# A two-layer mixture-of-experts kernel: the slot table by one-hot products, slots given out by age, fp32r transposes of gathered rows

## The chip, the cores and the metric

The kernel runs on one core of a Trainium2 chip. The metric is device time in microseconds (us): the median of three runs, 1536.97 us for the kernel before (1535.93 to 1539.32). One more execution was profiled; all rows below are from it.

## The reference

Two layers over 512 tokens of width 1024, all in fp32. Each layer mixes tokens (two kinds of attention, then an output projection), normalises, and runs 16 experts, of which each token uses two. The experts are what the change touches:

```python
def grouped_moe(x, w_router, router_bias, exp_w_gate, exp_w_up, exp_w_down):
    xf = x.reshape(b * s, d)                                   # 512 x 1024
    scores = sigmoid(einsum('nd,de->ne', xf, w_router))        # 512 x 16
    biased = scores + router_bias
    group_score = lax.top_k(biased.reshape(n, 4, 4), 2)[0].sum(-1)
    in_group = (arange(16) // 4)[None, :] == argmax(group_score, -1)[:, None]
    _, idx = lax.top_k(where(in_group, biased, -inf), 2)       # two experts a token
    w = take_along_axis(scores, idx, -1); w = w / w.sum(-1, keepdims=True)
    combine = sum(one_hot(idx, 16) * w[..., None], axis=1)
    y = zeros_like(xf)
    for e in range(16):
        h = silu(xf @ exp_w_gate[e]) * (xf @ exp_w_up[e])      # 1024 -> 512, twice
        y = y + combine[:, e:e + 1] * (h @ exp_w_down[e])      # 512 -> 1024
    return y
...
for l in range(2):
    x = layer_norm(alpha * x + token_mixer(x, ...), ln1_g[l], ln1_b[l])
    x = layer_norm(alpha * x + grouped_moe(x, ...), ln2_g[l], ln2_b[l])
```

The kernel computes an expert for its own tokens only: up to 128 of them, packed into one tile.

## The kernel before

**Products.** An fp32 product is made of three fp32r products (`mm3`, L454): each operand is split into a high part, cast by ACT (L484), and a low part, the rest subtracted by DVE (L495). An expert has 12 weight loads of 512 KB (128x1024), so 12 casts and 12 subtractions of 128x1024 stand beside its products: gate and up (24 records of 128x512 each per 512 outputs, 48 in all) and down.

**Routing.** The output projection yields the four tiles of 128 tokens one after the other. For each, `route_tile` (L1095) picks the two experts on DVE as one-hot rows `oh`, and gets from small bf16 products on PE (weights `lstr`, `ones`) the rank of every token among its expert's tokens. Rank and expert make a row number `ri` of the slot table; two scatters on POOL (L1153) write token number and weight there, in the DRAM table `tabd`. `route_end` (L1164) counts the tokens of each expert, then reads 128 slots x 16 experts of the table back into SBUF by one DMA on SP's queue, into the tile `tb` (in the trace `m<-tabd`). `tb` gives expert e's token numbers and weights.

**Experts.** `moe` (L1240) runs them in order. Expert 0's tokens are fetched by a one-hot product on PE (into two PSUM banks, `xacc`), which needs no table. Experts 1 to 15 are gathered by an indirect DMA on POOL's queue (L1179) from `x1d` in DRAM with a column of `tb`; eight transposes on PE (L445) turn such a tile, ACT and DVE split it. The result of an expert is scaled and added into `zd` in DRAM by an indirect scatter (L1184), except the last one, which `ln2` adds by a one-hot product. `ln2` begins with four reads of `zd` on SP's queue (`s<-zd`). Behind expert 14 stands `overflow` (L1190), a conditional block for experts of more than 128 tokens; it is skipped with this data, yet its buffers and its DMAs' semaphores take part in the plan.

**Order and slots.** No order is written by hand. Operations are recorded, and `plan` (L175) plays them through a model of the engines: the planned start sets the order on each engine. It also gives every tile a slot: 48 slots of 4 KB (`s`), 56 small ones (`m`), 8 tiny ones (`t`), 4 + 4 PSUM banks (`p`, `a`). `take` (L269) sorts the free slots by the time at which they came free and, among those free at the planned time, picks the newest. A tile that gets a slot waits on the chip for every reader and writer of the tile before it there.

Of the kernel before, what the change touches and what calls it, by code (L numbers as in the profile page):

```python
# [22 lines left out]
P = 128  # L23
# [68 lines left out]
class Recorder:  # L92
# [82 lines left out]
    def plan(self):  # L175
# [93 lines left out]
        def take(o, t):  # L269
            for b in o.allocs:  # L270
                s = slots[b.kind]
                s.sort()
                i = max((j for j in range(len(s)) if s[j][0] <= t + 1e-9), default=0)
                b.slot = s.pop(i)[1]
                g = b.group
                if g is not None:
                    if live[g] >= self.QUOTA[g]:
                        heapq.heappop(glive[g])
                        live[g] -= 1
                    live[g] += 1  # L280
                    turn[g].pop()
# [138 lines left out]
class Chip:  # L420
# [13 lines left out]
    def mm(self, out, terms, start, stop, transpose=None, also=()):  # L434
        dt = {F: 4, FR: 1, BF: 1}
        n = self.n(out)
        if transpose is not None:
            dur = 0.11
        else:
            dur = sum(max(dt[x.dtype if not isinstance(x, View) else x.ap.dtype] * n, 256) / 2400 + 0.004 for _, x in terms)  # L440

        def fn():
            o = real(out)
            if transpose is not None:
                self.nc.tensor.transpose(o, real(transpose[0]), transpose[1])  # L445
            for i, (w, x) in enumerate(terms):
                self.nc.tensor.matmul(o, real(w), real(x), start=start and i == 0, stop=stop and i == len(terms) - 1)  # L447
        reads = [x for t in terms for x in t] + ([transpose[0]] if transpose else [])
        o = self.r.add("PE", dur, fn, [out], reads, allocs=also)
        o.cols = sum(n * w.shape[0] / P for w, _ in terms) + n * (transpose is not None)  # L450
        o.cnt = sum(2 if (x.ap.dtype if isinstance(x, View) else x.dtype) == F else 1 for _, x in terms) + (transpose is not None)
        return o
# [91 lines left out]
def build(tc, x0, xT0, w_idx, w_main, w_br, w_out, w_exp, bgate, idxg, idxb,  # L544
          ln1g, ln1b, ln2g, ln2b, wrt, rbias, ln1c, hconst, tab0, out):
    nc = tc.nc
    with ExitStack() as ctx:
# [19 lines left out]

        ident = const.tile([P, P], F, name="ident")
        make_identity(nc, ident)
        identb = const.tile([P, P], BF, name="identb")  # L570
# [23 lines left out]
        rowid = const.tile([P, P], F, name="rowid")  # L594
        nc.gpsimd.iota(rowid, pattern=[[NE, P]], base=1, channel_multiplier=0, allow_small_or_imprecise_dtypes=True)
        spacer = const.tile([1, 1], F, name="spacer")

# [6 lines left out]
        def sm(shape, dtype=F):  # L604
            return R.buf("m", shape, dtype)
# [9 lines left out]
        lnc = const.tile([P, DEPTH, 2, KD], F, name="lnc")  # L615
        onesf = const.tile([P, P], F, name="onesf")
        nc.vector.memset(onesf, 1.0)
# [60 lines left out]

        def transpose_tile(src, dst_of):
            for hb in range(2):  # L680
                ps = bank("a")
                for k in range(4):
                    c = (hb * 4 + k) * P
                    C.tr(ps[:, k * P:(k + 1) * P], src[:, c:c + P], ident)
                dst_of(hb, ps)
# [408 lines left out]

        def route_tile(t, rt, sc, scored, sels, oh0, xacc):  # L1095
            bi = sm([P, NE])
# [39 lines left out]
            else:  # L1136
                for f in later + [pick]:
                    f()
                later.clear()
            o2, ri = sm([P, 2, NE]), R.buf("t", [P, 2], I32)  # L1140
            C.tt(o2, oh, pr[:, None, :NE].to_broadcast([P, 2, NE]), OP.mult)
            C.v("reduce_max", ri, o2, axis=AX.X, n=2 * NE)
            ent, o3, w2, rw = R.buf("t", [P, 2, 2], I32), sm([P, 2, NE]), sm([P, 2]), sm([P, 2])
# [4 lines left out]
            C.v("reciprocal", rw[:, 1:2], rw[:, 0:1])  # L1148
            last = C.ts(ent[:, :, 1:2].bitcast(F), w2[:, :, None], rw[:, 1:2], 1.0 / ALPHA, OP.mult, OP.mult)
            for j in range(2):  # L1150
                def scatter(j=j):
# [11 lines left out]

        def route_end(sels):  # L1164
            pc = bank("a")
            for tt in range(NT):
                C.mm(pc[:, :NE], [(ones, sels[tt])], tt == 0, tt == NT - 1)
            mc, mci = sm([P, 1]), sm([P, 1], I32)
            C.v("reduce_max", mc, pc[:, :NE], axis=AX.X, n=NE)
            C.v("tensor_copy", mci, mc)  # L1170
            tb, gl = sm([P, NE, 2], I32), sm([P, 2], I32)
            o = C.dma(tb, tabd[0:P * NE, :].rearrange("(r e) w -> r e w", e=NE), P * 160, rtok=["tab0"])
            o.deps.update(table_writes)
            C.ts(gl[:, 0:1], tb[:, NE - 1, 0:1], float(S - 1), None, OP.min)
            return tb, gl, mci

# [13 lines left out]
        def overflow(l, mci):  # L1190
# [45 lines left out]

            o = R.add("ALL", 0.3, fn, reads=[mci], rtok=[f"x1{t}" for t in range(NT)] + ["tab0", "y"], allocs=bufs)
            written.append(o)

        def moe(l, tb, gl, mci, loads, xacc, until, routed):  # L1240
            def prep(e):
# [5 lines left out]
                if e == 0:  # L1247
# [4 lines left out]
                    return xh, xl  # L1252
                xg = s4([P, D], group="xg")
                last = e == NE - 1
                gather(xg, gl[:, 0:1] if last else tb[:, e, 0:1], [xh, xl], not last)
                transpose_tile(xg, dst)
                return xh, xl
# [31 lines left out]
            def down(e, sg):  # L1289
# [16 lines left out]
                def scaled(n, ps):  # L1306
                    C.mul(yo[:, half(n)], ps, tb[:, e, 1:2].bitcast(F))
                    if lo is not None:
                        C.stt(lo[:, half(n)], ps, tb[:, e, 1:2].bitcast(F), yo[:, half(n)].bitcast(F), OP.mult, OP.subtract)
                def whole(n):  # L1310
                    w = weights(e, 4 + n)
                    ps = bank("p")
                    product(ps, w, range(4))
                    scaled(n, ps)
                    if n:
                        add_rows(tb[:, e, 0:1], yo)
                if lo is None:
# [44 lines left out]
            oh, tf = s4([P, NT, P], FR), sm([P, NT])  # L1362
            C.stt(tf, tb[:, NE - 1, 0:1].to_broadcast([P, NT]), float(NE), tilerow, OP.mult, OP.add).deps.add(mark)
            for t in range(NT):
# [75 lines left out]
        for l in range(DEPTH):  # L1440
# [53 lines left out]
            table_writes.clear()  # L1494
            sels, oh0, xacc = [], s4([P, NT, P]), [bank("p") for _ in range(2)]
            caps = [(None, CAP0), (R.ops[-2], CAP1)]
            rw, rsum, rcon = router_rows(l)
            for t, r, sc, scored, until in out_proj(l, mts, pair, x0 if l == 0 else x2d, None if l == 0 else "x2", rw, rsum, rcon):
                if t == 0:
                    caps.append((until, CAP2))  # L1500
                routed = route_tile(t, r, sc, scored, sels, oh0, xacc)
            caps.append((until, None))
            tb, gl, mci = route_end(sels)
            tail = moe(l, tb, gl, mci, expert_loads(l, caps), xacc, caps[2][0], routed)
        ln2(DEPTH - 1, None, tail)
# [84 lines left out]
```

## Time and profile before

| | |
|---|---|
| runs | 1536.97 us, median of 3 (1535.93 to 1539.32) |
| profiled execution | 1539.54 us, its span 1537.7 us |
| PE busy | 1475.2 us (96%) |
| DVE busy | 1249.5 us (81%) |
| ACT busy | 896.6 us (58%) |
| POOL busy | 142.4 us (9%) |
| mean granted TensorE clock | 0.983 |

PE is busy but for 62.5 us of the span (1537.7 - 1475.2). The span outside is 1.84 us. In rows of the trace, `p` and `a` are PSUM banks, `s`, `m` and `t` the slot pools; `out<-in` names the tiles; a bracket at a row's end holds the idle time ahead of it and what ended it. PEclk 1.00 is 2.4 GHz, and a stretch between 0.5 and 1 holds times at 1.2 GHz. Experts run from about 449 to 750 us in layer 0 and from about 1210 to 1512 us in layer 1.

### The profile page before, as it was taken

The page shows a single profiled execution, that of the slowest core. Times are in us where ns is not written, and L with a number is a line of the kernel's source. Part 1 is how long each engine was busy: PE and PEld are TensorE (multiplying, and loading weights), DVE is VectorE, ACT ScalarE, POOL GpSimd, SP SyncE. Part 2 cuts the span into 40 slices and gives each one's busy share as a digit, 9 for nine tenths or more (in the row PEclk, how much of TensorE's full clock was granted, in tenths as well). Part 3 has the DMA queues.
Part 4 walks back from the last instruction along what each step waited for, and adds up shares of the span by engine and source line. Part 5 has one row for each costly group of instructions (what it writes and reads, how often), then busy time and mean ns, then how long its engine had stood idle before and what let it go on. Part 6 is the DMA issues. An engine that isn't in the chain of part 4 may idle for free. (4 is left out here: it accounts for less than half of the span.)

```text
span 1537.7 us, 21018 instructions
## 1 busy us (share of the span) xinstructions
PE 1475.2 (96%) x7188; PEld 1178.9 (77%) x7188; DVE 1249.5 (81%) x2301; ACT 896.6 (58%) x1459; POOL 142.4 (9%) x127
## 2 busy tenths in 40 slices
PE   8999999999989999999799999999999899999985
PEld 7877777777867878888588777777778578888874
DVE  5699996777587989999765999867766789999975
ACT  4335543675146878888623455446831478888873
POOL 0000000000031131210010000000001212112110
PEclk9999999999999999999999999999999899999998
DMA  6221112117888989999712221221287889999962
GB/s 217 71 91 57 68 56 89 63 42 288 302 280 297 337 309 348 341 334 333 237 61 69 83 61 50 82 83 55 70 306 279 302 307 351 341 352 339 351 216 108
DMA packets 91265, 308.52 MB, mean 201 GB/s; under 512 B 15439, under 2 KB 15567, under 8 KB 91152
## 3 DMA queue, kind: packets, MB, share of 16 engines
q1 hardware_dynamic: 82000, 290.69, 53.5%
q0 software_dynamic: 9152, 16.43, 4.5%
q8 instruction: 58, 0.95, 0.2%
q14 instruction: 55, 0.45, 0.1%
HBM read 293.80 MB, written 28.46 MB: 210 GB/s over the span
## 5 line engine op out<-in xcount | busy, mean ns | idle before, releaser
L447 PE MATMUL p<-s,s 128*128 128x512 f32 (+1 forms) x5192 | 1268.1, 398 | 28.1 <-DVE s L495 25.7
L447 PEld LDWEIGHTS p<-s,s 128*128 128x128 f32 x5192 | 952.9, 191 | 234.9 <-DVE s L495 25.5
L495 DVE TENSOR_TENSOR s<-s,s 128x1024 fp32r<-128x1024 f32 (+2 forms) x526 | 612.1, 1195 | 152.4 <-ACT s L484 112.3
L484 ACT CAST s<-s 128x1024 fp32r<-128x1024 f32 (+2 forms) x526 | 518.2, 1029 | 226.6 <-PE p L447 141.6
L495 DVE TENSOR_TENSOR s<-a,s 128x256 fp32r<-128x256 f32 (+3 forms) x386 | 169.5, 479 | 36.5 <-ACT s L484 32.7
L484 ACT CAST s<-a 128x256 fp32r<-128x256 f32 (+2 forms) x354 | 127.1, 414 | 109.8 <-PE a L445 103.7
L445 PE MATMUL a<-ident,s 128*128 128x128 f32 x888 | 134.0, 277 | 13.5 <-DMA s<-x1d,m 6.4
L445 PEld LDWEIGHTS a<-ident,s 128*128 128x128 f32 x888 | 106.7, 142 | 44.9 <-issue 11.5
L523 POOL TENSOR_TENSOR m<-m,nhalf 128x1 f32<-128x1 f32 x24 | 17.8, 741 | 891.0 <-DVE m L495 881.6
L480 ACT ACTIVATE s<-a 128x512 f32<-128x512 f32 (+3 forms) x156 | 61.9, 450 | 46.0 <-PE a L447 27.5
L484 ACT COPY s<-a 64x512 f32<-64x512 f32 (+1 forms) x48 | 27.8, 583 | 96.7 <-PE a L445 45.3
L1184 POOL DMA_INDIRECT zd<-s,m x30 | 61.1, 2035 | 199.8 <-ACT s L487 167.4
L487 ACT ACTIVATE s<-p,m 128x512 f32<-128x512 f32 (+1 forms) x64 | 44.1, 689 | 53.5 <-PE p L447 50.6
L1179 POOL DMA_INDIRECT s<-x1d,m x30 | 43.6, 1452 | 267.9 <-PE p L447 220.2
L464 PE MATMUL a<-s,s 64*128 64x384 f32 (+3 forms) x456 | 67.4, 351 | 0.0
L447 PEld LDWEIGHTS a<-s,s 128*128 128x128 f32 x360 | 57.0, 188 | 9.2 <-issue 2.2
L447 PE MATMUL a<-s,s 128*128 128x324 f32 (+4 forms) x360 | 62.2, 321 | 1.5 <-DVE s L495 1.3
L464 PEld LDWEIGHTS a<-s,s 64*128 64x128 f32 x456 | 41.3, 185 | 27.6 <-issue 20.4
L495 DVE MAX8 m<-s 128x8 f32<-128x256 f32 (+2 forms) x96 | 53.4, 556 | 1.8
L495 DVE MATCH_REPLACE8 s<-m,s 128x256 f32<-128x256 f32 (+2 forms) x96 | 52.0, 542 | 0.0
L495 DVE TENSOR_TENSOR_SCAN s<-s 128x128 f32<-128x128 f32 (+3 forms) x64 | 51.0, 812 | 0.1
L484 ACT CAST s<-p 128x512 fp32r<-128x512 f32 x48 | 27.9, 588 | 38.5 <-DVE p L495 22.7
(107 smaller groups left out, 632.4 us busy)
## 6 DMA issues: line engine op xcount, KB each, us to landing
s<-in_w_exp SPq DMA_DIRECT2D x384, 512.0 KB
s<-in_w_main SPq DMA_DIRECT2D x79, 512.0 KB
s<-in_w_br SPq DMA_DIRECT2D x16, 512.0 KB
s<-in_w_out SPq DMA_DIRECT2D x16, 512.0 KB
x1d<-s SPq DMA_DIRECT2D x8, 512.0 KB
zd<-s SPq DMA_DIRECT2D x8, 512.0 KB
s<-zd SPq DMA_DIRECT2D x8, 512.0 KB
s<-in_w_idx SPq DMA_DIRECT2D x8, 324.0 KB
```

The lines of the kernel that those rows point to most:

```text
L445: self.nc.tensor.transpose(o, real(transpose[0]), transpose[1])
L447: self.nc.tensor.matmul(o, real(w), real(x), start=start and i == 0, stop=stop and i == len(terms) - 1)
L464: self.nc.tensor.matmul(real(o), real(t[i][0]), real(t[i][1]), start=i == 0, stop=stop and i == len(t) - 1)
L480: self.nc.scalar.activation(real(out), real(src), func, bias=real(bias), scale=real(scale), **kw)
L484: return self.r.add("ACT", 0.1 + self.psum(out, src) + self.n(out) * 0.833e-3, lambda: self.nc.scalar.copy(real(out), real(src)), [out], [ ...
L487: return self.r.add("ACT", 0.2 + self.n(out) * 0.833e-3, lambda: self.nc.scalar.mul(real(out), real(src), real(c)), [out], [src, c])
L495: getattr(self.nc.vector, method)(real(out), *[real(a) for a in args], **{k: real(x) for k, x in kw.items()}, **({} if accum is None else ...
L523: return self.r.add("POOL", 0.47, lambda: self.nc.gpsimd.tensor_tensor(real(out), real(a), e, OP.pow), [out], [a])
L1179: R.add("POOL", 1.04, lambda: nc.gpsimd.indirect_dma_start(out=real(dst), out_offset=None, in_=x1d, in_offset=IOA(ap=real(idx), axis=0), * ...
L1184: rows = R.add("POOL", 1.04, lambda: nc.gpsimd.indirect_dma_start(out=zd, out_offset=IOA(ap=real(idx), axis=0), in_=real(src), in_offset=None,
```

## The change

Three edits. First, `take` gives out slots of all pools but `m` oldest first. Second, gathered tiles are declared fp32r and transposed by an fp32r identity: 8 transposes for each of 15 experts in 2 layers, 240 of the 888 transposes of L445. Third, the table is made in SBUF: each tile's one-hot rows over slot numbers (`slot`) and its token numbers and weights by expert (`vals`) are multiplied on PE, eight products a layer into one bank, and DVE turns the bank into `ti` (token numbers) and `tw` (weights). The read of `tabd` is gone; the scatters into `tabd` stay, and only the overflow block waits for them.

```diff
@@ take
-                i = max((j for j in range(len(s)) if s[j][0] <= t + 1e-9), default=0)
+                i = max((j for j in range(len(s)) if s[j][0] <= t + 1e-9), default=0) if b.kind == "m" else 0
@@ tr
-                self.nc.tensor.transpose(o, real(transpose[0]), transpose[1])
+                self.nc.tensor.transpose(o.bitcast(transpose[1].dtype), real(transpose[0]), transpose[1])
@@ constants
-        ident = const.tile([P, P], F, name="ident")
-        make_identity(nc, ident)
+        onesf = const.tile([P, P], F, name="onesf")
+        make_identity(nc, onesf)
+        identr = const.tile([P, P], FR, name="identr")
+        nc.vector.tensor_copy(identr, onesf)
+        ident = identr.bitcast(F)
...
+        tokoff = const.tile([P, NT], F, name="tokoff")
+        nc.gpsimd.iota(tokoff, pattern=[[P, NT]], base=-4 * S, channel_multiplier=1, allow_small_or_imprecise_dtypes=True)
@@ route_tile
-            o2, ri = sm([P, 2, NE]), R.buf("t", [P, 2], I32)
+            o2, rf, ri = sm([P, 2, NE]), sm([P, 2, 2]), R.buf("t", [P, 2], I32)
             C.tt(o2, oh, pr[:, None, :NE].to_broadcast([P, 2, NE]), OP.mult)
-            C.v("reduce_max", ri, o2, axis=AX.X, n=2 * NE)
+            C.v("reduce_max", rf[:, 0, :], o2, axis=AX.X, n=2 * NE)
+            C.stt(rf[:, 1, :], rf[:, 0, :], 1.0, idf, OP.add, OP.subtract)
+            C.tt(slot[:, 2 * t:2 * t + 2, :], rowid[:, None, :].to_broadcast([P, 2, P]), rf[:, 1, :, None].to_broadcast([P, 2, P]), OP.is_equal)
+            C.ts(vals[:, 2 * t:2 * t + 2, :NE], oh, tokoff[:, t:t + 1], None, OP.mult)
+            C.v("tensor_copy", ri, rf[:, 0, :])
...
+            C.tt(vals[:, 2 * t:2 * t + 2, NE:], oh, ent[:, :, 1:2].bitcast(F).to_broadcast([P, 2, NE]), OP.mult)
@@ route_end
-            tb, gl = sm([P, NE, 2], I32), sm([P, 2], I32)
-            o = C.dma(tb, tabd[0:P * NE, :].rearrange("(r e) w -> r e w", e=NE), P * 160, rtok=["tab0"])
-            o.deps.update(table_writes)
-            C.ts(gl[:, 0:1], tb[:, NE - 1, 0:1], float(S - 1), None, OP.min)
-            return tb, gl, mci
+            pt = bank("a")
+            for i in range(2 * NT):
+                C.mm(pt[:, :2 * NE], [(slot[:, i, :], vals[:, i, :])], i == 0, i == 2 * NT - 1).deps.add(scored)
+            ti, tw, gl = sm([P, NE], I32), sm([P, NE]), sm([P, 2], I32)
+            C.ts(ti, pt[:, :NE], 4.0 * S, None, OP.add)
+            C.v("tensor_copy", tw, pt[:, NE:2 * NE])
+            C.ts(gl[:, 0:1], ti[:, NE - 1:NE], float(S - 1), None, OP.min)
+            return ti, tw, gl, mci
@@ overflow
+            o.deps.update(table_writes)
@@ moe, prep
-                xg = s4([P, D], group="xg")
+                xg = s4([P, D], FR, group="xg")
-                gather(xg, gl[:, 0:1] if last else tb[:, e, 0:1], [xh, xl], not last)
-                transpose_tile(xg, dst)
+                gather(xg.bitcast(F), gl[:, 0:1] if last else ti[:, e:e + 1], [xh, xl], not last)
+                transpose_tile(xg, dst, identr)
```

How the order moves shows at three places. The first is PE behind the routing of layer 0. `s36` holds `vals`, `s9` is `slot`, `p0` and `p1` are expert 0's `xacc`, `p2` is its gate product. Now:

```order
L447 MATMUL a2_4467<-s36_4262,s9_4253 128x32 x4
L447 MATMUL p0_4368<-s21_3647,s35_4233 128x512
L447 MATMUL p1_4381<-s21_3647,s35_4233 128x512
L447 MATMUL a2_4467<-s36_4262,s9_4253 128x32 x2
L447 MATMUL a0_4497<-k0_4372,onesf_84 128x32
L447 MATMUL a2_4467<-s36_4262,s9_4253 128x32 x2
L445 MATMUL a3_4503<-identr_89,s28_4486 128x128 x4
L447 MATMUL a0_4497<-k0_4372,onesf_84 128x32 x7
L445 MATMUL a1_4540<-identr_89,s28_4486 128x128 x4
L447 MATMUL p2_4548<-s40_4457,s5_4532 128x512
```

The table's products stand among the last one-hot products of `xacc`; in the kernel before there is nothing in their place. Further on PE, at the end of expert 0's up product, before (`s34` and `s31` are the gathered tiles of experts 1 and 2, `s37` is expert 0's hidden tile, `p0_4661` expert 1's gate product):

```order
L447 MATMUL p0_4546<-s28_4563,s33_4474 128x512
L447 MATMUL p0_4546<-s32_4532,s33_4474 128x512
L445 MATMUL a2_4614<-ident_84,s37_4550 128x128 x4
L445 MATMUL a0_4626<-ident_84,s34_4552 128x128 x4
L445 MATMUL a1_4633<-ident_84,s34_4552 128x128 x4
L445 MATMUL a2_4641<-ident_84,s31_4572 128x128 x4
L445 MATMUL a3_4646<-ident_84,s31_4572 128x128 x4
L447 MATMUL p0_4661<-s22_4583,s11_4554 128x512
```

and now (`p3_4598` is expert 0's up product, `s27` and `s8` the gathered tiles, `s29` the hidden tile):

```order
L447 MATMUL p3_4598<-s9_4589,s30_4510 128x512
L445 MATMUL a2_4623<-identr_89,s27_4534 128x128 x4
L445 MATMUL a3_4630<-identr_89,s27_4534 128x128 x4
L447 MATMUL p3_4598<-s36_4602,s5_4532 128x512
...
L447 MATMUL p3_4598<-s13_4614,s30_4510 128x512
L445 MATMUL a1_4657<-identr_89,s8_4556 128x128 x4
L445 MATMUL a0_4669<-identr_89,s8_4556 128x128 x4
L445 MATMUL a2_4681<-identr_89,s29_4621 128x128 x4
L447 MATMUL p0_4689<-s20_4654,s35_4536 128x512
```

Expert 1's transposes moved into the middle of expert 0's up product, 12 of its 24 records ahead of its end. The second place is DVE at the last tile of layer 0's routing, before (`t5` is `ri`, `s14_4229` the one-hot rows for expert 0, `s5` its token rows; a 128x1024 row is a weight subtraction):

```order
L495 TENSOR_SCALAR s14_4229<-rowid_113,m52_4434 128x128 [waits DVE_49]
L495 TENSOR_REDUCE t5_4439<-m49_4436 128x2 [waits DVE_49]
L495 TENSOR_TENSOR s34_4448<-s7_3621,s41_4432 128x1024 [waits DMAHW3_49,DMAHW4_49,PE_49,Activation_49]
L495 TENSOR_TENSOR s32_4455<-s24_3626,s28_4446 128x1024 [waits Activation_49]
L495 TENSOR_REDUCE m50_4472<-a0_4307 128x1 [waits PE_49]
L495 COPY s5_4453<-p3_4385 128x512
L495 CAST m55_4486<-m50_4472 128x1 [waits DVE_49]
L495 TENSOR_TENSOR s14_4488<-a1_4465,s33_4474 128x512 [waits Activation_49]
L495 TENSOR_TENSOR s38_4495<-s6_3734,s42_4460 128x1024
L495 TENSOR_TENSOR s14_4488<-a0_4490,s33_4474 128x512 [waits Activation_49]
```

and now (`s9` is `slot`, `t7` is `ri`, `m49_4513` is `ti`, `m53` is `tw`, `s28` the token rows of expert 0):

```order
L495 TENSOR_REDUCE m45_4471<-a1_4453 128x1 [waits PE_49]
L495 TENSOR_REDUCE m49_4474<-m46_4463 128x2 [waits DVE_49]
L495 CAST m43_4478<-m45_4471 128x1 [waits DVE_49]
L495 SCALAR_TENSOR_TENSOR m49_4474<-m49_4474,m53_4432 128x2 [waits DVE_49]
L495 TENSOR_TENSOR s6_4483<-s27_3624,s40_4457 128x1024 [waits Activation_49]
L495 TENSOR_TENSOR s9_4253<-rowid_115,m49_4474 128x256 [waits DVE_49]
L495 CAST t7_4492<-m49_4474 128x2
L495 TENSOR_TENSOR s33_4495<-s8_3629,s13_4481 128x1024 [waits Activation_49]
L495 TENSOR_SCALAR m49_4513<-a2_4467 128x16 [waits DVE_49,PE_49]
L495 COPY m53_4520<-a2_4467 128x16
L495 TENSOR_SCALAR m45_4524<-m49_4513 128x1 [waits DVE_49]
L495 COPY s28_4486<-p1_4381 128x512
```

The copy of expert 0's token rows comes after `ti` and `tw`, which wait for the table's products. The third place is DVE behind the skipped overflow block of layer 0, before:

```order
L495 TENSOR_TENSOR s19_7391<-s43_7095,s32_7268 128x1024 [waits DMAHW5_49,Activation_49]
L495 TENSOR_TENSOR s44_7401<-s25_7107,s41_7393 128x1024 [waits DMASW4_49,DMAHW6_49,PE_49,Activation_49]
L495 TENSOR_TENSOR s43_7417<-s2_7232,s45_7399 128x648 [waits DMASW7_49,DMASW3_49,DMAHW5_49,DVE_49,Activation_49]
L495 TENSOR_TENSOR s35_7432<-s47_7127,s10_7415 128x1024 [waits DMASW3_49,DMAHW7_49,PE_49,Activation_49]
L495 TENSOR_TENSOR s46_7407<-s46_7407,p3_7403 128x256 [waits PE_49]
```

and now:

```order
L495 TENSOR_TENSOR s14_7429<-s36_7098,s23_7304 128x1024 [waits DMAHW3_49,DVE_49,Activation_49]
L495 TENSOR_TENSOR s40_7439<-s34_7118,s38_7431 128x1024 [waits DMAHW4_49,PE_49,Activation_49]
L495 TENSOR_TENSOR s11_7453<-s41_7133,s12_7437 128x1024 [waits DMAHW5_49,PE_49,Activation_49]
L495 TENSOR_TENSOR s15_7466<-s26_7256,s4_7311 128x648 [waits DMAHW4_49,DVE_49,PE_49]
L495 TENSOR_TENSOR s45_7478<-s19_7145,s32_7458 128x1024 [waits DMAHW6_49,PE_49,Activation_49]
...
L495 TENSOR_TENSOR s13_7529<-s21_7190,s20_7505 128x1024 [waits DMAHW1_49,DMASW2_49,Activation_49]
```

The waits on POOL's DMA semaphores (`DMASW`) ahead of these subtractions went, and the first is now on a later row.

## Rows read from the trace of the kernel before

**Rows 1.** stages of the span: length, busy time of each engine, PEclk, DMA share

```profile
core 0: us, PE busy (x) PEld busy (x) DVE busy (x) ACT busy (x) POOL busy (x), PEclk, DMA share, GB/s
432.00:450.00 18.00, 15.24 (x66) 8.92 (x67) 15.15 (x64) 7.08 (x10) 6.31 (x10) 0.91 0.99 360
450.00:470.00 20.00, 17.09 (x73) 13.87 (x72) 16.42 (x20) 13.74 (x17) 3.94 (x3) 0.83 0.60 195
...
520.00:600.00 80.00, 77.43 (x347) 63.52 (x346) 69.35 (x68) 63.52 (x77) 18.65 (x9) 0.96 0.95 327
600.00:700.00 100.00, 100.00 (x479) 83.60 (x478) 93.34 (x92) 85.58 (x103) 18.19 (x11) 1.00 0.99 343
...
735.00:760.00 25.00, 17.89 (x83) 13.41 (x81) 16.86 (x23) 14.45 (x21) 0.03 (x1) 0.93 0.64 215
...
1215.00:1245.00 30.00, 25.89 (x119) 21.09 (x118) 21.45 (x23) 18.58 (x23) 5.39 (x4) 0.94 0.84 277
...
1400.00:1500.00 100.00, 94.73 (x452) 78.96 (x451) 87.53 (x90) 79.23 (x95) 16.47 (x9) 0.98 0.87 299
```

**Rows 2.** timeline of all engines, layer 0, 438 to 470 us; releaser in brackets

```profile
439.63 0.19 DVE L495 TENSOR_REDUCE t<-m 128x2 int32<-128x32 f32 x1 [0.88 <-DMA tabd<-t,t]
...
445.94 1.65 PE L447 MATMUL a<-k,onesf 128*128 128x32 f32 x14
...
448.61 11.17 PE L447 MATMUL p<-s,s 128*128 128x512 f32 x48 [0.56 <-DVE s L495]
...
451.25 0.33 SPq L526 DMA_DIRECT2D m<-tabd  x1
...
455.00 1.94 POOL L1179 DMA_INDIRECT s<-x1d,m  x1 [8.36 <-DVE m L495]
...
462.90 1.94 PE L445 MATMUL a<-ident,s 128*128 128x128 f32 x8 [1.68 <-DMA s<-x1d,m]
...
466.88 3.39 PE L447 MATMUL p<-s,s 128*128 128x512 f32 x9
```

**Rows 3.** timeline of PE, the same place in layer 1

```profile
1209.67 11.18 PE L447 MATMUL p<-s,s 128*128 128x512 f32 x48 [0.27 <-DVE s L495]
1222.39 1.50 PE L445 MATMUL a<-ident,s 128*128 128x128 f32 x12 [1.54 <-DMA s<-x1d,m]
1226.46 0.90 PE L445 MATMUL a<-ident,s 128*128 128x128 f32 x5 [2.57 <-DMA s<-x1d,m]
1227.02 5.26 PE L447 MATMUL p<-s,s 128*128 128x512 f32 x15
```

**Rows 4.** timelines of DVE, PE and SP, end of the experts of layer 0

```profile
739.72 1.23 DVE L495 TENSOR_TENSOR s<-s,s 128x1024 fp32r<-128x1024 f32 x1 [3.15 <-DMA zd<-s,m]
...
741.33 3.48 PE L447 MATMUL p<-s,s 128*128 128x256 f32 x18 [3.87 <-DVE s L495]
...
742.48 2.47 SPq L526 DMA_DIRECT2D s<-zd  x4
```

**Rows 5.** timelines of DVE and PE, end of the experts of layer 1

```profile
1498.12 3.68 DVE L495 TENSOR_TENSOR s<-s,s 128x1024 fp32r<-128x1024 f32 x3 [6.45 <-DMA zd<-s,m]
...
1499.40 3.36 PE L447 MATMUL p<-s,s 128*128 128x256 f32 x14 [5.12 <-DVE s L495]
```

**Rows 6.** waits of the whole span: us, times, longest

```profile
ACT s L484 <- DMA zd<-s,m: 17.0, 10, 6.6
```

**Rows 7.** DMA issues: KB each (where known), median us to landing

```profile
zd<-s,m POOLq DMA_INDIRECT x30, 9.2
```

**Rows 8.** lines by form, PEld and DVE: count, busy us, mean ns, idle before

```profile
L447 PEld LDWEIGHTS p<-s,s 128*128 128x128 f32 x5192 | 952.9, 191 | 234.9 <-DVE s L495 25.5 <-issue 15.5 <-ACT s L484 10.0
L445 PEld LDWEIGHTS a<-ident,s 128*128 128x128 f32 x888 | 106.7, 142 | 44.9 <-issue 11.5 <-DVE s L495 9.6 <-DMA s<-x1d,m 3.4
L447 PEld LDWEIGHTS <-identb 128*128 128x128 bf16 x72 | 5.8, 99 | 11.4 <-issue 8.7 <-DVE m L495 0.3
...
L495 DVE TENSOR_TENSOR s<-s 128x256 f32<-128x256 f32 x8 | 3.3, 414 | 0.0
```

More of the change, by code (lines that the diff above doesn't have):

```diff
@@ L615, in build @@
         lnc = const.tile([P, DEPTH, 2, KD], F, name="lnc")
-        onesf = const.tile([P, P], F, name="onesf")
         nc.vector.memset(onesf, 1.0)
@@ L677, in normalize, with transpose_tile @@
                 C.stt(dst[:, half(n)], dst[:, half(n)], rstd, b[:, half(n)], OP.mult, OP.add)
-        def transpose_tile(src, dst_of):
+        def transpose_tile(src, dst_of, by=ident):
             for hb in range(2):
@@ L683, in transpose_tile @@
                     c = (hb * 4 + k) * P
-                    C.tr(ps[:, k * P:(k + 1) * P], src[:, c:c + P], ident)
+                    C.tr(ps[:, k * P:(k + 1) * P], src[:, c:c + P], by)
                 dst_of(hb, ps)
@@ L1093, in router_rows, with route_tile @@
             return w[:, 0, :, :], sums[:, 0, :], sums[:, 1, :]
-        def route_tile(t, rt, sc, scored, sels, oh0, xacc):
+        def route_tile(t, rt, sc, scored, sels, oh0, xacc, slot, vals):
             bi = sm([P, NE])
@@ L1162, in build, with route_end @@
         scatters, table_writes, picks, later, written = [], [], [], [], []
-        def route_end(sels):
+        def route_end(sels, slot, vals, scored):
             pc = bank("a")
             for tt in range(NT):
-                C.mm(pc[:, :NE], [(ones, sels[tt])], tt == 0, tt == NT - 1)
+                C.mm(pc[:, :NE], [(ones, sels[tt])], tt == 0, tt == NT - 1).deps.add(scored)
             mc, mci = sm([P, 1]), sm([P, 1], I32)
@@ L1237, in overflow, with moe @@
             o = R.add("ALL", 0.3, fn, reads=[mci], rtok=[f"x1{t}" for t in range(NT)] + ["tab0", "y"], allocs=bufs)
+            o.deps.update(table_writes)
             written.append(o)
-        def moe(l, tb, gl, mci, loads, xacc, until, routed):
+        def moe(l, ti, tw, gl, mci, loads, xacc, until, routed):
             def prep(e):
@@ L1306, in scaled @@
                 def scaled(n, ps):
-                    C.mul(yo[:, half(n)], ps, tb[:, e, 1:2].bitcast(F))
+                    C.mul(yo[:, half(n)], ps, tw[:, e:e + 1])
                     if lo is not None:
-                        C.stt(lo[:, half(n)], ps, tb[:, e, 1:2].bitcast(F), yo[:, half(n)].bitcast(F), OP.mult, OP.subtract)
+                        C.stt(lo[:, half(n)], ps, tw[:, e:e + 1], yo[:, half(n)].bitcast(F), OP.mult, OP.subtract)
                 def whole(n):
@@ L1315, in whole @@
                     if n:
-                        add_rows(tb[:, e, 0:1], yo)
+                        add_rows(ti[:, e:e + 1], yo)
                 if lo is None:
@@ L1362, in moe @@
             oh, tf = s4([P, NT, P], FR), sm([P, NT])
-            C.stt(tf, tb[:, NE - 1, 0:1].to_broadcast([P, NT]), float(NE), tilerow, OP.mult, OP.add).deps.add(mark)
+            C.stt(tf, ti[:, NE - 1:NE].to_broadcast([P, NT]), float(NE), tilerow, OP.mult, OP.add).deps.add(mark)
             for t in range(NT):
@@ L1495, in build @@
             sels, oh0, xacc = [], s4([P, NT, P]), [bank("p") for _ in range(2)]
+            slot, vals = s4([P, 2 * NT, P]), s4([P, 2 * NT, 2 * NE])
             caps = [(None, CAP0), (R.ops[-2], CAP1)]
@@ L1500, in build @@
                     caps.append((until, CAP2))
-                routed = route_tile(t, r, sc, scored, sels, oh0, xacc)
+                routed = route_tile(t, r, sc, scored, sels, oh0, xacc, slot, vals)
             caps.append((until, None))
-            tb, gl, mci = route_end(sels)
-            tail = moe(l, tb, gl, mci, expert_loads(l, caps), xacc, caps[2][0], routed)
+            ti, tw, gl, mci = route_end(sels, slot, vals, scored)
+            tail = moe(l, ti, tw, gl, mci, expert_loads(l, caps), xacc, caps[2][0], routed)
         ln2(DEPTH - 1, None, tail)
```

## The prediction

> **What bounds the kernel now.** I read the stages first [rows 1]. In the middle of an expert phase PE is busy all of the time (100.00 of 100 us at full clock), DVE 93.34 of 100 close behind, and the DMA share is 0.99. Nothing that saves PE no work can gain there. What can be gained is at the edges: 432 to 470 and 1215 to 1245, where routing hands over to the experts, 735 to 760 and the end of 1400 to 1500, where the experts end, and one hole in 520 to 600. The PEclk column belongs to the reading: each of these stretches also stands at 0.83 to 0.98, so a stall there is paid twice, once in idle time and once in records that run at 1.2 GHz afterwards. The timelines of these places [rows 2 to 5] name what PE waited for, and the waits by engine [rows 6] say how much of that is the landing of a scatter.
>
> The handover in layer 0 [rows 2] is a chain: the read of the table is issued at 451.25, when the last scatter into it has landed; POOL, idle for 8.36 us, issues expert 1's gather at 455.00; PE, which began expert 0 at 448.61, stands ready before the rows land and transposes at 462.90. At the two ends [rows 4, 5], DVE is kept from a weight subtraction by "DMA zd<-s,m" for 3.15 and 6.45 us, and PE behind it for 3.87 and 5.12 us: the subtraction writes a slot that the overflow block or a late scatter held, given to it because it was the newest free.
>
> **Table path, layer 0.** What is lost now: expert 0 takes 11.17 us from 448.61 for its 48 records; 20 transposes (4 of its own, 8 for each of two gathers) take 2.5 us at the 1.50 us for 12 [rows 3]; so expert 1's gate could start at 462.28. It starts at 466.88, a loss of 4.6. The clock is 0.83 over 450 to 470, which is 3.4 us of clock; most of it falls on the wait, and I count 1.2 for the records after 466.88. Together 5.8.
>
> What the change does: no read and no wait for scatters, so the gather is issued when `ti` is there. In the order `ti` follows the last tile's `slot` and a weight subtraction. DVE gets, for each tile, one 128x256 comparison at 0.41 us [rows 8] and four small instructions at about 0.19 (the 128x32 row in [rows 2]): 1.2 us, 4.7 in the layer, and 0.4 for `ti` and `tw`. In 432 to 450 DVE was busy 15.15 of 18 us, so 2.85 were free: of the 3.5 us of the first three tiles 0.7 stay over. With the last tile's 1.2 and the 0.4 DVE is 2.2 late. Off that goes the 0.88 us wait for a `t` slot [rows 2], which an oldest-first choice removes: 1.3 late. The copy of expert 0's rows stands behind `ti` in DVE's queue, so expert 0 itself starts about 1.3 us later, near 449.9. PE's 16 new records cost 1.9 us by the 1.65 for 14 of the same width [rows 2]; they stand where PE waits for DVE (15.24 busy of 18), so I count nothing for them; without that cover, 1.9 in a layer.
>
> Is the gather then in time? Issued near 448.5, and with the 7.9 us from 455.00 to 462.90, its rows are there at 456.4. PE wants them after 36 of expert 0's 48 records, 8.4 us behind its start: 458.3. Two microseconds to spare; expert 2's gather, issued 2 us later, is wanted 3.7 us later. Net gain 5.8 - 1.3 = 4.5. Bounds: 5.8 where DVE's additions vanish in its waits, 0 where the gather lands 4.5 us later than that.
>
> **Table path, layer 1.** By the same count [rows 3]: 1209.67 + 11.18 + 2.5 = 1223.35 against 1227.02, 3.7 lost, and 0.94 over 30 us of clock [rows 1], 1.8 us, of which I take 1.7. Against 5.4 stand DVE's 2.2 less some idle time: net 3.5 (0 to 5.4). Both layers 8.
>
> **Oldest-first slots.** At the end of layer 0's experts the rows in the order show DVE's first subtractions behind the overflow block without a wait for POOL's DMAs. What goes is the 3.15 us and, of the clock (0.93 over 25 us, 1.75), some 1.5: 4.7. What is late next is `ln2`: its reads of `zd` are issued at 742.48 [rows 4] and wait for expert 14's scatter whatever the slots. I take 4 (0 to 4.7). At the end of layer 1 the gap is 5.12 us [rows 5], and the clock of 1400 to 1500 is 0.98, 2.0 us: 6.5 of 7.1 (0 to 7.1).
>
> Inside the phase, ACT waits 17.0 us for landing scatters, ten times, at most 6.6 [rows 6]. The longest lies in 520 to 600, where PE lacks 2.57 of 80 us and 3.2 us of clock: 5.8 us. Oldest-first moves each reuse about, but with 48 slots nearly all in use it can't move it far. Bounds 0 and 5.8; since a scatter's slot is reused at about the same distance in the first experts, I take 1, near the lower.
>
> Weight loads of the mixers also start earlier; none of the holes that I read lies there, so I count nothing, and harm would show as waits for `in_w_main`.
>
> **fp32r transposes.** 240 of 888. A transpose by the f32 identity has a weight load of 142 ns on average, an fp32r product's weight load 191, a bf16 identity's 99 [rows 8]. The bounds are 240 x 0.043 = 10.3 us of gain by the bf16 row and 240 x 0.049 = 11.8 us of loss by the fp32r row. They stand at like distances on both sides of the f32 transpose's own 142, so I keep that row's price and take nothing. The Trainium skill, in "TensorE: Matmul & The Clock Gate", section "Weight-path perf modes — Fast Weight Load (FWL) and DoubleRow", says that the fast load is on for 128 weights of a type other than FP32. By that rule fp32r tiles would load fast and the 10.3 us be gained; the trace disagrees so far, its fp32r loads being no faster than any.
>
> **Sum.** 4.5 + 3.5 + 4 + 6.5 + 1 + 0 = 19.5 us off the profiled execution's 1539.54: 1520.0. That execution lies 2.57 us above the median of the runs, 1536.97; off the median the sum gives 1517.5. I forecast 1518.
>
> **Rivals.** *Half of it is given back.* What PE gains at the handover it loses at the next thing that is late: loads (the DMA share in 600 to 700 is 0.99, and an earlier start eats the lead that 450 to 470 at 0.60 let build up), or `ln2` on `zd`. For it: DVE at 93% and DMA at 99%. Against it: in 600 to 700 PE never waits for either. Only half the gain stays: 1537 - 9.7 = 1527.
>
> *The transposes get cheap.* By the bf16 row, 1518 - 10.3 = 1508. For it speaks that the operand type changes; against it the 191 ns row, by which they would cost 11.8 us instead (1530).
>
> *The table doesn't come sooner.* `ti` waits behind the last tile's chain on DVE and the gather queues with loads at a DMA share of 0.99 in 432 to 450. If it lands 4.5 us later than counted, PE stalls in the middle of an up product, the clock falls as before, and the 8 are gone; if `ln2` also eats the ends, nothing is left: 1535.
>
> *Slower: scatters' slots come round too soon.* A scatter lands 9.2 us after its issue [rows 7], and holds its slot so long. Oldest-first hands out all slots in turn, so every expert's result tile comes back to a weight split after the same number of tiles. If that is about an expert's time or less, it happens at each scatter and no longer by chance. The hole in 520 to 600 prices one such hit at 5.8 us. From four hits on it decides: 4 x 5.8 = 23 us against 19.5, so 1541 with four. For it: the wait is there today, ten times. Against it: most of the ten cost PE little, with 100.00 us busy in 600 to 700, and a turn through 48 slots should be longer on average than the newest slot's.
>
> **How the numbers follow.** Forecast 0.55, with an own range of 1511 to 1525; half given back 0.17; cheap transposes 0.10; nothing left 0.09; slower 0.09. The range leaves out the slow case and a part of the cheap one: 1506 to 1536. A change of 0.2% (3 us) is about what measurement can tell from none. Faster than that: the forecast, half of it, the cheap transposes and a third of nothing left, 0.85. The same: the rest of nothing left, 0.06. Slower: 0.09.
>
> **What would show it.** Right: no `m<-tabd`; gathers issued near 448 and 1210; expert 1's transposes inside expert 0's up product with no wait of over 1 us for "DMA s<-x1d,m"; PEclk 1.00 in what is now 450 to 470; no wait of DVE for "DMA zd<-s,m" at the ends; the transposes by the identity unchanged at 142 ns of weight load. Wrong: PE stalled in expert 0's up product, new waits of ACT or DVE for scatters or for `in_w_exp`, `ln2` waiting for `s<-zd` by as much as the ends gained, or twelve transposes in clearly less than 1.50 us at the same clock.

## The result and the profile after

The changed kernel takes 1516.29 us, the median of 4 runs (1514.89 to 1519.07), beside 1538.14 for the kernel before (4 runs, 1535.93 to 1541.99). The ratio is 0.9858, 95% interval 0.9832 to 0.9883. The forecast was 1518. The profiled execution took 1516.78 us, its span is 1515.1. PE's idle time fell from 62.5 to 46.9 us (1515.1 less 1468.2 busy), and its busy time by 7.0 us.

The stages of the changed kernel, cut at its own marks (length, busy time of each engine, PEclk, DMA share):

```profile
core 0: us, PE busy (x) PEld busy (x) DVE busy (x) ACT busy (x) POOL busy (x), PEclk, DMA share, GB/s
434.50:450.90 16.40, 15.85 (x75) 9.93 (x75) 14.99 (x76) 5.39 (x8) 6.82 (x11) 0.79 0.97 364
450.90:470.00 19.10, 17.95 (x89) 14.02 (x87) 15.85 (x18) 13.20 (x16) 4.42 (x3) 1.00 0.86 307
470.00:520.00 50.00, 46.70 (x208) 36.00 (x207) 39.12 (x40) 37.40 (x45) 7.38 (x5) 0.97 0.86 289
520.00:600.00 80.00, 77.94 (x363) 64.07 (x363) 72.90 (x71) 66.97 (x80) 18.53 (x9) 1.00 0.97 344
600.00:700.00 100.00, 100.00 (x484) 83.51 (x483) 93.52 (x94) 84.04 (x104) 15.96 (x11) 1.00 1.00 361
733.00:753.00 20.00, 16.58 (x83) 12.32 (x81) 16.42 (x24) 12.51 (x19) 0.00 (x0) 1.00 0.76 283
1203.00:1233.00 30.00, 28.15 (x135) 21.44 (x133) 24.13 (x25) 22.86 (x28) 2.71 (x2) 1.00 0.91 304
1400.00:1478.00 78.00, 77.85 (x380) 64.99 (x379) 72.74 (x76) 66.60 (x83) 11.97 (x7) 1.00 0.87 309
```

Against [rows 1] the gaps at the two ends are smaller: 733 to 753 lacks 3.42 us of PE at full clock where 735 to 760 lacked 7.11 at 0.93, and 1400 to 1478 is full but for 0.15. The handover runs at full clock (450.9 to 470), but the stretch ahead of it (434.5 to 450.9) has 0.79 where 432 to 450 had 0.91. And 470 to 520 now lacks 3.30 us of PE at a clock of 0.97; in the kernel before it lacked 0.71 at full clock:

```profile
470.00:520.00 50.00, 49.29 (x233) 39.96 (x232) 42.22 (x42) 39.08 (x47) 7.41 (x5) 1.00 0.96 333
```

520 to 600 lacks 2.06 us, where it lacked 2.57. The handover in layer 0, all engines, answers to [rows 2]:

```profile
448.73 0.17 DVE L495 TENSOR_SCALAR m<-a 128x16 int32<-128x16 f32 x1 [0.25 <-PE a L447]
...
449.62 0.96 POOL L1162 DMA_INDIRECT tabd<-t,t  x1 [0.21 <-issue]
...
450.88 8.46 PE L447 MATMUL p<-s,s 128*128 128x512 f32 x36
450.88 1.67 POOL L1191 DMA_INDIRECT s<-x1d,m  x1 [0.30 <-ACT s L484]
...
459.17 0.79 PE L445 MATMUL a<-identr,s 128*128 128x128 f32 x8
459.80 3.00 PE L447 MATMUL p<-s,s 128*128 128x512 f32 x12
...
463.99 0.47 PE L447 MATMUL p<-s,s 128*128 128x512 f32 x1
...
468.78 2.90 PE L447 MATMUL p<-s,s 128*128 128x512 f32 x11 [0.67 <-DVE s L495]
```

`ti` is there at 448.73, 6 us ahead of the old gather; the new gather goes only at 450.88, behind the last scatter in POOL's queue. Expert 0 starts at 450.88. Expert 1's rows are in time: its transposes stand in the up product with no wait, and its gate product starts at 463.99, where it was 466.88. The last row shows who is late next: DVE, with the weight splits of expert 1. Then the holes in 470 to 600, on ACT and PE:

```profile
496.99 2.94 ACT L484 CAST s<-s 128x1024 fp32r<-128x1024 f32 x3 [2.54 <-DMA zd<-s,m]
...
498.09 0.49 PE L447 MATMUL p<-s,s 128*128 128x512 f32 x1 [0.97 <-ACT s L484]
...
499.35 4.38 PE L447 MATMUL p<-s,s 128*128 128x512 f32 x11 [0.77 <-DVE s L495]
...
518.65 4.85 ACT L484 CAST s<-s 128x1024 fp32r<-128x1024 f32 x5 [3.11 <-DMA zd<-s,m]
...
519.75 0.49 PE L447 MATMUL p<-s,s 128*128 128x512 f32 x1 [1.11 <-ACT s L484]
...
521.01 2.79 PE L447 MATMUL p<-s,s 128*128 128x512 f32 x11 [0.77 <-DVE s L495]
...
540.08 2.94 ACT L484 CAST s<-s 128x1024 fp32r<-128x1024 f32 x3 [3.73 <-DMA zd<-s,m]
```

ACT waits for "DMA zd<-s,m" before a weight cast, three times in experts 2 to 5, and PE stands still twice each time, for the cast and for the subtraction after it (the third time for 0.54 and 0.76 us). Both ends of the expert phases, PE and SP, answer to [rows 4, 5]:

```profile
736.35 2.06 PE L447 MATMUL p<-s,s 128*128 128x256 f32 x15 [0.51 <-DVE s L495]
...
735.76 1.76 SPq L526 DMA_DIRECT2D s<-zd  x4
```

```profile
1480.49 2.42 PE L447 MATMUL p<-s,s 128*128 128x256 f32 x18 [0.52 <-DVE s L495]
...
1479.87 1.76 SPq L526 DMA_DIRECT2D s<-zd  x4
```

The gaps of 3.87 and 5.12 us are 0.51 and 0.52, and the reads of `zd` are issued 6.7 us earlier in layer 0 without holding `ln2` up. The waits of the whole span, to set beside [rows 6]:

```profile
POOL s L1191 <- DMA zd<-s,m: 14.4, 2, 7.5
ACT s L484 <- DMA zd<-s,m: 13.3, 6, 3.7
```

### The profile page after: what moved, and what is told of

Read it like the earlier page. It is cut to its first block, busy times and chain, and to the rows that moved or that the text cites. A ratio compares the mean times of both kernels' runs of the same rounds, so it can differ in the third digit from the quotient of the medians.

```text
span 1515.1 us, 21052 instructions
## 1 busy us (share of the span) xinstructions
PE 1468.2 (97%) x7220; PEld 1171.4 (77%) x7220; DVE 1247.5 (82%) x2346; ACT 890.2 (59%) x1459; POOL 140.0 (9%) x128
## 5 line engine op out<-in xcount | busy, mean ns | idle before, releaser
L495 DVE TENSOR_TENSOR s<-s,s 128x1024 fp32r<-128x1024 f32 (+1 forms) x526 | 606.6, 1192 | 84.4 <-ACT s L484 73.9
L484 ACT CAST s<-s 128x1024 fp32r<-128x1024 f32 (+1 forms) x526 | 515.5, 1034 | 64.0 <-PE p L447 26.0
L480 ACT ACTIVATE s<-a 128x512 f32<-128x512 f32 (+3 forms) x156 | 61.9, 451 | 112.8 <-PE a L464 69.1
L445 PE MATMUL a<-identr,s 128*128 128x128 f32 x888 | 122.7, 267 | 4.5 <-DVE s L495 3.4
L445 PEld LDWEIGHTS a<-identr,s 128*128 128x128 f32 x888 | 101.2, 141 | 33.1 <-issue 9.1
L1196 POOL DMA_INDIRECT zd<-s,m x30 | 54.6, 1821 | 262.4 <-ACT s L487 184.4
L447 PEld LDWEIGHTS a<-s,s 128*128 128x128 f32 x392 | 61.4, 189 | 6.7 <-issue 1.4
L447 PE MATMUL a<-s,s 128*128 128x324 f32 (+5 forms) x392 | 66.4, 316 | 0.0
L1191 POOL DMA_INDIRECT s<-x1d,m x30 | 47.0, 1567 | 192.9 <-PE p L447 109.2
```

What stands on the lines that cost most here:

```text
L445: self.nc.tensor.transpose(o.bitcast(transpose[1].dtype), real(transpose[0]), transpose[1])
L480: self.nc.scalar.activation(real(out), real(src), func, bias=real(bias), scale=real(scale), **kw)
L484: return self.r.add("ACT", 0.1 + self.psum(out, src) + self.n(out) * 0.833e-3, lambda: self.nc.scalar.copy(real(out), real(src)), [out], [ ...
L495: getattr(self.nc.vector, method)(real(out), *[real(a) for a in args], **{k: real(x) for k, x in kw.items()}, **({} if accum is None else ...
L1191: R.add("POOL", 1.04, lambda: nc.gpsimd.indirect_dma_start(out=real(dst), out_offset=None, in_=x1d, in_offset=IOA(ap=real(idx), axis=0), * ...
L1196: rows = R.add("POOL", 1.04, lambda: nc.gpsimd.indirect_dma_start(out=zd, out_offset=IOA(ap=real(idx), axis=0), in_=real(src), in_offset=None,
```

## The experiments

Medians in us; before stands for the kernel before on the same chip: 1537.03 beside the first four runs, 1535.37 beside the next four, 1535.6 beside the last. These three groups ran on different chips, so two kernels of different groups are compared by their ratios to the kernel before. Each expectation was written before its run; A and B in it are rival theories.

**One edit alone.** Three kernels, each the kernel before with one edit of the change.

```diff
# oldest-first slots
-                i = max((j for j in range(len(s)) if s[j][0] <= t + 1e-9), default=0)
+                i = max((j for j in range(len(s)) if s[j][0] <= t + 1e-9), default=0) if b.kind == "m" else 0
# the table (with slot, vals, ti and tw as in the change)
-            o = C.dma(tb, tabd[0:P * NE, :].rearrange("(r e) w -> r e w", e=NE), P * 160, rtok=["tab0"])
...
+                C.mm(pt[:, :2 * NE], [(slot[:, i, :], vals[:, i, :])], i == 0, i == 2 * NT - 1).deps.add(scored)
# fp32r (with identr as in the change)
-                xg = s4([P, D], group="xg")
+                xg = s4([P, D], FR, group="xg")
-                transpose_tile(xg, dst)
+                transpose_tile(xg, dst, identr)
```

> The kernel before with oldest-first slots alone. Theory A (the parts add up): the two waits for POOL's DMAs at the ends of the expert phases go, 5 and 6.5 us, and other slot waits move about by 2 us either way: 9 to 13 us off the kernel before, ratio 0.992 to 0.994. Rival B (the ends are held by the reads of zd as long as the table path keeps the phase late): under 5 us, ratio above 0.997.

Measured 1519.01, ratio 0.9861 (0.9834 to 0.9889): 18 us, more than theory A had.

> The kernel before with the one-hot table alone (newest-first slots, f32 transposes). Theory A: expert 1's gate product begins 3 to 5 us earlier in each layer and this lasts to the end: 5 to 9 us off, ratio 0.994 to 0.997. Rival B: what the earlier start gains is given back at the ends, where the newest-free slots make DVE wait for scatters all the same: 0 to 3 us off, ratio above 0.998.

Measured 1529.32, ratio 0.9941 (0.9920 to 0.9962): 7.7 us, theory A.

> The kernel before with fp32r transposes of the gathered rows alone. Theory A: in the trace of the changed kernel a block of 12 transposes costs PE 1.29 us from record to record, against 1.46 before; 30 blocks by 0.17 are 5.1 us, ratio 0.9967. Rival B: PE gains it and waits it out at the next weight split of DVE: under 1 us, ratio above 0.999.

Measured 1533.15, ratio 0.9971 (0.9952 to 0.9989): 3.9 us, close to theory A's 5.1. Here are 12 transposes and the record after them on PE, first of the kernel before in a second trace, then of this one (start, us):

```profile
544.38 1.47 PE L445 MATMUL a<-ident,s 128*128 128x128 f32 x12
545.61 16.62 PE L447 MATMUL p<-s,s 128*128 128x512 f32 x72
```

```profile
614.96 1.23 PE L445 MATMUL a<-identr,s 128*128 128x128 f32 x12
616.02 16.59 PE L447 MATMUL p<-s,s 128*128 128x512 f32 x72
```

From the first transpose to the next product it was 1.23 us and is 1.06. Eight of the twelve are fp32r, four (the hidden tile's) still f32. That is 0.17 us for each of 30 gathered tiles, 5.1 in all. The three savings sum to 29.6 us, where the whole change has 19 to 22: the parts do not add up. Most of why is in the last section.

**One edit undone.** First newest-first slots in the changed kernel:

```diff
-                i = max((j for j in range(len(s)) if s[j][0] <= t + 1e-9), default=0) if b.kind == "m" else 0
+                i = max((j for j in range(len(s)) if s[j][0] <= t + 1e-9), default=0)
```

> The changed kernel with newest-first slots again. Theory A: 9 to 13 us above the changed kernel, so a ratio to the kernel before of 0.992 to 0.994, and the waits of DVE for POOL's DMAs at the ends of the expert phases are back with 3 to 7 us each. Rival B (the parts work only together): nearly all is lost, ratio above 0.997.

Measured 1525.95, ratio 0.9921 (0.9895 to 0.9947), 9.7 above the 1516.27 of the changed kernel, 8.4 by the ratios. Theory A, at its lower edge: PE's gap at the end of layer 0's experts is back, and larger than in [rows 4], with PE there 10 us earlier:

```profile
731.16 4.59 PE L447 MATMUL p<-s,s 128*128 128x256 f32 x20 [4.84 <-DVE s L495]
```

DVE waits 6.6 us for a scatter there; in layer 1 it is ACT that does, for 4.5.

The other two undo the table (`tb` and its read of `tabd` as before) and the fp32r transposes (the fp32r lines above, reversed); the changed kernel ran beside them.

> The changed kernel itself, beside the three kernels that follow: its ratio to the kernel before was 0.986, and both theories expect that again, 0.984 to 0.988.

Measured 1516.27, ratio 0.9866 (0.9839 to 0.9892).

> The changed kernel without the one-hot table (the table is read back from DRAM; oldest-first slots and fp32r transposes stay). Theory A (the table's 4 us at each handover stay to the end): 8 us above the changed kernel. Rival B (with oldest-first slots most of it is lost again inside experts 1 to 4, where ACT waits for scatters to land at 497, 518 and 541 us): 0 to 3 us above it.

Measured 1516.11, ratio 0.9863 (0.9835 to 0.9891): rival B. With the other two edits in place, the table by products is worth nothing that can be measured. Its waits show the exchange: the transposes wait for the gather again, and ACT waits less for scatters, between 470 and 570 us only 1.5 us where the changed kernel has 9.4.

```profile
PE a L445 <- DMA s<-x1d,m: 5.4, 4, 2.4
ACT s L484 <- DMA zd<-s,m: 10.3, 5, 2.6
```

> The changed kernel with f32 transposes of the gathered rows. Theory A (PE paces the phase, a block of 12 transposes costs 0.17 us more): 5 us above the changed kernel. Rival B (hidden behind DVE's splits): within 1 us of it.

Measured 1521.44, ratio 0.9902 (0.9879 to 0.9925): 5.2 above, theory A, and the size that the transposes' rows give. The two intervals overlap, but the runs do not: the lowest of this kernel is 1520.49, the highest of the changed kernel beside it 1520.10.

**The waits for scatters.** What eats the table's gain should be the three holes. This kernel leaves the change as it is and tells the planner that a scatter's source slot is held 6 us longer than it reckons:

```diff
+HOLD = 6.0
-                b.last = max(b.last, o.end + self.LAT)
+                b.last = max(b.last, o.end + self.LAT + (HOLD if o in self.late else 0.0))
...
+            R.late.add(rows)          # in add_rows
```

> The changed kernel, with a plan that counts the source tile of a scatter into zd as held for 6 us more, so that its slot is given out later; nothing else is changed. Theory A (the holes of PE at 497, 518 and 541 us come from slots given out before the scatter has landed, and cost 5 to 7 us in the first four experts): the waits of ACT for zd fall from 13.3 us to under 4, and the kernel is 4 to 8 us below the changed one. Rival B (a later release makes the loads late, since 48 slots are nearly all in use): no gain, or up to 5 us above.

Measured 1509.38 (1508.51 to 1512.26), ratio 0.9829 (0.9802 to 0.9855), 6.9 below the changed kernel beside it: theory A, and the fastest kernel of the study. Here too the intervals overlap, but only one of its five runs (1512.26) is above one of the six of the changed kernel (1511.77). No split waits for a scatter any more; of the waits for `zd` this alone is left, POOL's queue ahead of a gather:

```profile
POOL s L1192 <- DMA zd<-s,m: 7.9, 1, 7.9
```

and the stretches that held the holes are full (columns as above):

```profile
490.00:530.00 40.00, 40.00 (x192) 32.64 (x191) 36.98 (x38) 34.91 (x43) 6.71 (x4) 1.00 0.99 356
530.00:600.00 70.00, 70.00 (x332) 58.07 (x331) 66.92 (x66) 61.99 (x74) 16.10 (x8) 1.00 1.00 360
```

**What the hold leaves.** Three variants of it: without the table (the table's lines above reversed), with newest-first slots (the line of the undone edit above), and with a longer hold:

```diff
-HOLD = 6.0
+HOLD = 12.0
```

> The kernel with the longer hold of scatter sources, without the one-hot table (read back from DRAM). Theory A (the table's 4 us a layer were eaten by scatter waits in experts 1 to 4 and come through once these are gone): 6 to 9 us above the kernel with the hold (1509.4), so 1515 to 1518, like the changed kernel without a table and without the hold. Rival B (the table never gains anything at the end): within 2 us of the kernel with the hold.

Measured 1512.64, ratio 0.9843 (0.9814 to 0.9871), 3.3 above the hold, 2.2 by the ratios: between the two theories. The intervals and the runs overlap, so that this gain is likely and not shown; the marks below show where it would be.

> The kernel with the longer hold, and newest-first slots in place of oldest-first. Theory A (oldest-first also keeps the slots of the skipped overflow block, whose semaphores end with the last scatters, from the first splits behind it): DVE waits for POOL's DMAs at the ends again, 4 to 10 us above the kernel with the hold. Rival B (the hold alone does it, the order in which slots are given out is indifferent): within 2 us of it.

Measured 1527.53, ratio 0.9947 (0.9923 to 0.9970), 18 above: theory A in kind, larger than expected. The waits of ACT and DVE for scatters are back, all three of them at the ends:

```profile
ACT s L484 <- DMA zd<-s,m: 14.3, 2, 7.4
DVE s L495 <- DMA zd<-s,m: 6.7, 1, 6.7
```

Whether the slots waited for are those of the overflow block or those of late scatters, no run separates.

> The kernel with a hold of 12 us in place of 6. Theory A (at 6 us no split waits for a scatter any more, so more gains nothing): within 2 us of it. Rival B (the longer hold keeps two slots more from the loads): 2 to 6 us above.

Measured 1513.85, ratio 0.9848 (0.9815 to 0.9880), 4.5 above, 2.9 by the ratios. Undecided: the intervals overlap, no split of this kernel waits for a scatter, but POOL's gathers wait for them for 25.6 us where it was 7.9:

```profile
POOL s L1192 <- DMA zd<-s,m: 25.6, 3, 9.4
```

**The hole at 556.**

> The kernel before once more, for a second trace. Theory A (the hole of PE at 556 us, with the 7.45 us scatter at 540, was an accident of the one profiled execution): no hole of over 1 us between 540 and 570, and the rest of the phase as before. Rival B (it belongs to the slots of the kernel before): the hole is there again, some 2.5 us of idle time and PEclk below 1 behind it.

One run, 1531.78. Theory A: PE runs through 545.61 to 562 with 72 records without a gap (the second row of the pair above), and POOL's scatter at that place took 1.77 us:

```profile
540.19 1.77 POOL L1184 DMA_INDIRECT zd<-s,m  x1 [5.04 <-DMA s<-in_w_exp]
```

In the traces of the three single edits and of the changed kernel no scatter of layer 0 holds POOL for more than 2.6 us, and the time from expert 5's Silu to expert 6's, 23.75 us in the first trace (544.65 to 568.40), is 17.68 in this one (544.58 to 562.26). So the hole was, by these traces, an accident of one execution, and cost it 6 us.

## Why the prediction was right, and where it was not

The table gives the start, in us, of an expert's one Silu on ACT (`L480 ACTIVATE s<-p`) and of `ln2`'s first product by the identity on PE, in five traces.

| mark | before | before again | changed | hold | hold, no table |
|---|---|---|---|---|---|
| layer 0, expert 1 | 473.71 | 472.72 | 471.72 | 471.22 | 474.76 |
| expert 6 | 568.40 | 562.26 | 568.24 | 559.86 | 561.10 |
| expert 14 | 709.89 | 703.76 | 708.10 | 699.76 | 700.93 |
| `ln2` | 752.68 | 747.49 | 746.03 | 737.73 | 740.85 |
| layer 1, expert 1 | 1234.37 | 1225.88 | 1221.12 | 1213.80 | 1223.40 |
| expert 14 | 1468.04 | 1458.78 | 1452.62 | 1445.13 | 1450.87 |
| `ln2` | 1512.47 | 1504.71 | 1490.53 | 1482.29 | 1488.80 |

*Ends of the expert phases, 4 and 6.5 us.* Right in place, cause and size. From expert 14's Silu to `ln2` layer 0 took 42.79 us and takes 37.93; layer 1 took 44.43 and takes 37.91: 4.9 and 6.5 (against the second trace of before, 5.8 and 8.0). The undone edit brings the gap back. In every trace with oldest-first slots this stretch takes 37.0 to 39.9 us in either layer, and 42.8 to 47.8 in those of the kernel before, of the other two single edits and of the undone edit. The rival that `ln2` would wait for `zd` instead did not happen.

*Table path, 4.5 and 3.5 us.* The step was right, its place in the end was not. Expert 0 started later and expert 1's gate 2.9 us earlier; of the 2.27 us by which expert 0 was late, 1.0 was there before the routing began (the `k` product at 420.00 stood at 421.03). The gather went at 450.88 and not near 448.5, since the forecast had no scatter ahead of it in POOL's queue; the two microseconds to spare, and the later start of expert 0, covered that. But the sum counted these 8 us as lasting. Without the holes, the table is 3.5 us ahead at expert 1 (474.76 against 471.22), 1.2 at experts 6 and 14: most of what is gained at the handover goes to the splits of the next experts, as the late DVE row at 468.78 shows. Layer 1 shows the same: counted from the lead of 3.1 at the first `ln2`, 6.5 us are gained by expert 1, of which 2.6 are left at expert 14. At the last mark the trace with the table is 6.5 us ahead in all, by the medians and ratios 2 to 3. With the holes nothing is left of it.

*Inside the phase, 1 us.* Wrong twice. The 5.8 us hole that priced it was an accident, so its going is no work of the change. And some slots that the change gives out were not free in time: from expert 1 to 6 the changed kernel falls from 1.0 us ahead of the second trace of the kernel before to 6.0 behind, 7 us. This is the rival "scatters' slots come round too soon", in its mechanism: three hits of some 2.3 us, below the four hits at 5.8 from which it was to decide. The hold, which changes only when the plan takes a scatter's source for free, gave 6.9 us back.

It took two edits together to make these holes. From expert 1's Silu to expert 6's in layer 0 the traces with oldest-first slots and the table take 96.52 and 95.89 us (the changed kernel, twice) and 96.89 (without fp32r); those with one of the two or neither take 86.3 to 89.5, but for the 94.69 of the execution with the accident, and the hold, which has both, 88.64. These 7 to 8 us are most of what the parts fail to add up by, and by the medians too the table gains nothing on top of oldest-first slots: the ratio is 0.9861 without it and 0.9902 with it, or 0.9863 and 0.9866 with fp32r as well.

*fp32r transposes, 0.* Wrong by some 5 us. I compared weight loads, and the term rested on the row of 142 ns. The loads of the changed kernel are as long as before (none of the 888 is under 137 ns):

```profile
L447 PEld LDWEIGHTS p<-s,s 128*128 128x128 f32 x5192 | 948.0, 189 | 235.7 <-DVE s L495 27.1 <-issue 14.9 <-ACT s L484 10.7
L445 PEld LDWEIGHTS a<-identr,s 128*128 128x128 f32 x888 | 101.2, 141 | 33.1 <-issue 9.1 <-DVE s L495 3.9 <-ACT s L484 2.1
```

Yet fp32r transposes follow one another more closely than f32 ones. This shows at every expert once nothing is late: from expert 6's Silu to expert 14's in layer 0 it is 141.4 to 141.5 us in all five traces with f32 transposes of the gathered rows and 139.8 to 140.0 in all nine with fp32r ones, 0.2 us an expert, so some 6 for 30 experts; the medians give 5.2 in the changed kernel. By the medians alone it can't be seen in one pair, oldest-first slots without the table (0.9861 as f32, 0.9863 as fp32r), and that stays open. In the rows that I chose stood the time of a block, 1.50 us for 12 from the first start to the last end, but nothing on fp32r to set beside it. The Trainium skill ("TensorE: Matmul & The Clock Gate", section "Weight-path perf modes — Fast Weight Load (FWL) and DoubleRow") says that the fast weight load is on for 128 weights of a type other than FP32. The trace does not show it for fp32r: half of the 10.3 us priced for it came, but with the transposes' loads at 141 ns and fp32r products' at 189.

So the total was met in part by luck, and two of the prediction's own signs of being wrong came with it: new waits of ACT for scatters, and twelve transposes in clearly less than 1.50 us (1.22 in the changed kernel). The two profiled executions without the accident are 15.0 us apart (1531.78 and 1516.78), and 13.8 of these come at the ends (5.8 and 8.0). Little of the table's 8 us lasted, 7 us were lost in holes where I had 1 of gain, and the transposes gave 5 where I had none; the accident, by which the execution that I subtracted from was 6 us longer, I had reckoned in part as the change's gain and in part, 2.6, scaled away. Open remains why oldest-first slots alone gain 18 us by the medians, where their trace is 10.7 ahead of the second trace of before at the last mark (1494.04 against 1504.71): the kernel before varied by 11 us over its 18 runs beside them (1532.04 to 1542.84), and what its slower runs met has no trace but the hole at 556. Open too is whether 12 us of hold is worse than 6.

## What to carry to other kernels

A slot allocator needs the time at which a buffer is really free: for the source of an indirect scatter that is the landing, which this plan put at 7.8 us after the issue or a little later (`ROWS` in the kernel) where the changed kernel's median is 9.6, and 6 us more in the plan were worth 6.9 us, about as much as the whole table edit by itself. A gain at a handover counts only if the engine that is late next has slack there; follow it to the end of the stage before adding it up. And before a stall is made a term of a sum, look for it in a second trace.

## What the hardware showed that I had not expected

Transposes of 128x128 tiles typed fp32r through an fp32r identity cost PE 0.17 us less per eight than f32 ones, 21 ns each, with weight loads of unchanged length. A scatter of an expert's rows held POOL for 1.6 to 2.6 us in layer 0 of the traces looked at, but once for 7.45, and that execution lost 6 us there. With the newest free slots given out first, splits behind the skipped conditional block waited up to 7.4 us for the last scatters; that the slots were those of the block's buffers is argued and not shown.
